# Matrix products of two feature blocks taken by turns, so that the PSUM bank changes

## The chip, the cores and the metric

The kernel runs on one core of a Trainium2 chip. The metric is the time of one execution on the device in microseconds (us), as the median of the runs shown. The engines of a core work side by side, each through its own queue in order: TensorE (PE in the profile; its weight loads are PEld), VectorE (DVE), ScalarE (ACT), GpSimd (POOL) and SyncE (SP), which issues the DMA transfers here. TensorE writes its products to PSUM, a memory of 8 banks in each partition, where they are summed.

## The reference

The reference is a decoder trunk of two layers on 256 positions of 1024 features, in float32. Cut to what matters:

```python
def swiglu(h, w_gate_up, w_down):
    a, b = jnp.split(h @ w_gate_up, 2, axis=-1)
    return (jax.nn.silu(a) * b) @ w_down

def hybrid_layer(x, ...):
    x = x + 0.5 * swiglu(rms_norm(x, ffn1_norm), ffn1_w_gate_up, ffn1_w_down)   # D_FF = 2816
    h = rms_norm(x, mix_norm)
    z = h @ w_in                                     # u, q, k, v and the logits gl of two gates
    u, q, k, v, gl = ...
    y_pool = multiscale_pool(u, pool_w, pool_scale)
    y_attn = moba_attention(rope(rms_norm(q)), rope(rms_norm(k)), v)            # 8 heads of 64
    gates = jax.nn.sigmoid(gl + b_gate).reshape(B, S, 2, D)
    merged = gates[:, :, 0] * (y_pool @ w_branch_pool) + gates[:, :, 1] * (y_attn @ w_branch_attn)
    x = x + merged @ w_out
    return x + 0.5 * swiglu(rms_norm(x, ffn2_norm), ffn2_w_gate_up, ffn2_w_down)
```

Nearly all of the work is in products of activations with weights that are read once.

## The kernel before

**Split operands.** Each float32 operand is split into a high part (rounded to the type that TensorE multiplies, float32r) and a low part (the rest, also float32r). A product of weights w and activations x is then hi(w)·hi(x) + hi(w)·lo(x) + lo(w)·hi(x). The activations' two parts lie side by side: `hx[:, k]` (also `hk[k]`) holds, for the feature block k of 128 features, 256 positions of the high part and then 256 positions of the low part. So one product with hi(w) and 512 moving columns gives two of the three terms, and one with lo(w) and 256 columns the third. In what follows they are the **high** and the **low** product. `chain` (L130) issues both, the high one into the whole of a PSUM bank (512 float32 in each partition), the low one into its first half, on top. At the end of a sum the two halves of the bank are added by `drain` (L157): ACT copies the second half (L158), and DVE adds the first (L159).

**Units.** The weights come in units of 128 x 2048, 16 blocks of 128 x 128. `unit()` (L91) starts the DMA of a unit into `raw` (4 buffers) and splits it in two halves of 8 blocks: for each half ACT writes hi (L112) and DVE writes lo (L113). There are six buffers for hi and six for lo, so three units fit, and a half's buffer is filled again once TensorE has read it for the last time. `blk(z, b)` picks the block b, in half 0 for b below 8 and in half 1 otherwise.

**Stages.** A layer is: a feed-forward stage (22 up units, then 11 down units), the mixing stage (tokens q, k, v, the projection u, 8 gate units with the attention between them, the branches, the output projection) and a second feed-forward stage. In an up unit the 16 blocks are two output blocks (j = 0 for the gate, j = 1 for the up part) times eight feature blocks k; the block is 2k + j. A gate unit has the same form, with the two gates as j. `pair` (L148) runs such a unit: it takes a PSUM tile `ps` of two banks, `ps[:, 0]` and `ps[:, 1]`, one for each j (there are two such tiles), goes over k and, within it, over j with `columns` (L142), and then drains. With `other` given, some other work is put between the first `at` feature blocks and the rest; that is so once in the first feed-forward stage and in the first gate of each layer. The first three up units of the kernel run together in `pairs` (L161), and in the other three feed-forward stages the first two up units are interleaved by hand; these do not go through `pair` without `other`.

In the down projection (L327 to L339) all 22 pairs of products of one output block go into one bank. The branches and the output projection use `chain3` (L135), three products of 256 columns for each block.

TensorE's instructions keep the order in which they are written (`mm`, L79, line 80 of the profile). The profile's line for all of them is L80, so the tiles tell them apart: `ps<-hx,hi` is a high product of an up, gate or u unit, `ps<-hx,lo` a low one, `ps<-ga,hi` and `ps<-gb,hi` belong to the down projection.

**Around it in the up projection.** For each unit DVE has two lo splits (L113), the drain's sum (L159), the scaling by the row factor (L322), the gate product (L325) and the low part of the result (L176); ACT has two hi splits (L112), the drain's copy (L158), the Silu (L324) and the high part of the result (L175).

Of the kernel before, what the change touches and what calls it, by code (L numbers as in the profile page):

```python
# [29 lines left out]
NK = D // P  # L30
# [19 lines left out]
def trunk_kernel(ctx: ExitStack, tc: tile.TileContext, x_in, w_in, pw_in, qkn_in, rope_in, mask_in, band_in, out):  # L50
# [28 lines left out]
    def mm(*args, **kw):  # L79
        return keep(nc.tensor.matmul(*args, **kw))  # L80

    def banks(pool, name):

        return pool.tile([P, 2, 2, S], F32, name=name, tag="mm" if pool is pmm else "at2")
# [30 lines left out]
    def blk(z, b, n=1):  # L115

        c = b * P % HALF
        return z[b * P // HALF][:, c:c + n * P]

    def steps(z):  # L120

        if len(z.shape) == 3:
            z = z.rearrange("p a s -> p (a s)")
        return z.rearrange("p (s a c) -> p a s c", a=4, c=4)

    def prod(ps, w, xk, first, last):

        return mm(steps(ps), lhsT=w, rhs=steps(xk), start=first, stop=last)

    def chain(ps, hi, lo, b, xk, first, last):  # L130

        prod(ps, blk(hi, b), xk, first, False)
        return prod(ps[:, 0, :], blk(lo, b), xk[:, 0, :], False, last)
# [8 lines left out]
    def columns(w, ps, ks):  # L142

        for k in ks:
            for j in range(2):
                chain(ps[j] if isinstance(ps, list) else ps[:, j], *w, 2 * k + j, hk[k], k == 0, k == NK - 1)

    def pair(w, t, other=None, at=0):  # L148

        ps = banks(pmm, "ps")  # L150
        columns(w, ps, range(at))
        if other:
            other()
        columns(w, ps, range(at, NK))
        drain(t, ps)

    def drain(t, ps):  # L157
        act(t, ps[:, :, 1, :], AF.Copy)  # L158
        tt(t, ps[:, :, 0, :], t, op=OP.add)  # L159
# [47 lines left out]
    hk = [hx[:, k] for k in range(NK)]  # L207
# [76 lines left out]
    def ffn(after, n0=0, end=False):  # L284
# [15 lines left out]
        if n0:  # L300
            pairs([unit() for _ in range(n0)], [wide() for _ in range(n0)])
            pair(unit(), wide(), sums, NK // 2)
        else:
            ws = [unit() for _ in range(2)]
            ts = [wide() for _ in range(2)]
            pss = [banks(pmm, "ps") for _ in range(2)]
            for u, k0, k1 in ((0, 0, NK - 1), (1, 0, 2), (0, NK - 1, NK), (1, 2, 4)):
                columns(ws[u], pss[u], range(k0, k1))
            drain(ts[0], pss[0])
            sums()  # L310
            columns(ws[1], pss[1], range(4, NK))
            drain(ts[1], pss[1])
        done = 0
        for i in range(n0 + 1 if n0 else 2, NF + 1):
            if i < NF:
                pair(unit(), wide())

            todo = range(done, min(done + 2, i) if i < NF else NF)
            done = todo.stop
            for j in todo:  # L320
                ab = abs_[j][1]
                tt(ab, ab, bc2(r[0]), op=OP.mult)  # L322
                sg = small.tile([P, S], F32, name="sg", tag="sg", bufs=2)
                act(sg, ab[:, 0, :], AF.Silu)  # L324
                tt(sg, sg, ab[:, 1, :], op=OP.mult)  # L325
                halves(gs[j], sg)
# [131 lines left out]
    def mix(l, after):  # L458
# [20 lines left out]
        def gate(f, *other):  # L479
            pair(unit(), gates[:, f], *other)  # L480
# [272 lines left out]
```

## Time and profile before

| | |
|---|---|
| median of 3 runs | 1010.97 us |
| lowest and highest run | 1008.93 and 1013.57 us |
| span of the profiled execution, first to last instruction | 1008.4 us |
| time of the profiled execution outside its span | not listed; the median of the runs lies 2.6 us above the span |
| TensorE, busy | 1001.3 us (99%), 6348 products |
| weight loads, busy | 905.9 us (90%) |
| DVE, busy | 795.9 us (79%) |
| ACT, busy | 626.1 us (62%) |
| HBM | 190 GB/s over the span |

A group's row reads: line, engine, operation, tile written and tiles read, shape, count, then busy us and the mean ns of one instruction, then the idle time of the engine just before them and what ended it. Products overlap in the array: one lasts 383 ns while the next starts 220 ns after it, so a count of starts per time says more than busy time. A row of the timeline has the start in us, the duration in us, engine, line, operation and tiles; in brackets the idle time before it and what ended that. A row of windows has the stretch, its length, and the busy time with the count of instructions for PE, PEld, DVE, ACT and POOL, then the granted clock of TensorE, the share of the DMA engines, and GB/s.

### The profile page before, as it was taken

How to read it: one execution, taken by the hardware profiler on the slowest of the kernel's cores; microseconds unless marked ns; L12 is line 12 of the kernel's file. 1: busy time of each engine (PE TensorE's matmuls, PEld its weight loads, DVE VectorE, ACT ScalarE, POOL GpSimd, SP SyncE). 2: the span in 40 equal slices, each digit the busy share in tenths (PEclk: the TensorE clock that was granted, in tenths of full speed). 3: DMA queues.
4: the chain of work that ended last, by engine and by line, in shares of the span. 5: the costliest groups of instructions: out<-in, count | busy, mean ns of one | idle time of the engine just before them, and what ended most of it. 6: DMA issues, size and time to landing. Idle time of an engine off the chain costs nothing.

```text
span 1008.4 us, 16031 instructions
## 1 busy us (share of the span) xinstructions
PE 1001.3 (99%) x6348; PEld 905.9 (90%) x6348; DVE 795.9 (79%) x1195; ACT 626.1 (62%) x985; POOL 1.4 (0%) x26
## 2 busy tenths in 40 slices
PE   8999999999999999999999999999999999999998
PEld 7889889898899998898898898898988998989987
DVE  7898866699769788886678888666998798888752
ACT  7966655567766766665576666556676567665641
POOL 0000000000000000000000000000000000000000
PEclk9999999999999999999999999999999999999999
DMA  8766566545526566656646565655544375656640
GB/s 290 272 229 218 180 209 209 192 156 169 204 84 227 192 209 209 209 174 206 206 168 211 206 209 175 207 203 186 189 167 147 118 255 173 228 181 209 207 148 22
DMA packets 30459, 192.91 MB, mean 191 GB/s; under 512 B 3376, under 2 KB 5680, under 8 KB 7856
## 3 DMA queue, kind: packets, MB, share of 16 engines
q1 hardware_dynamic: 30240, 191.71, 55.8%
q8 instruction: 50, 0.82, 0.3%
q10 hardware_dynamic: 144, 0.18, 0.1%
q14 instruction: 25, 0.20, 0.1%
HBM read 190.82 MB, written 1.05 MB: 190 GB/s over the span
## 4 chain that ended last, share of the span: by engine, by line
PE 84%; DVE 9%; ACT 3%; issue 2%; DMA 1%; SPq 0%; ACTq 0%; DVEq 0%
PE ps L80 73%; PE pt L80 6%; PE two L80 4%; DVE lo L113 3%; ACT hi L112 1%; DMA raw<-w 1%; DVE gates L159 1%; ACT pr L427 1%; DVE gates L483 1%; DVE nb L422 1%; DVE pr L432 1%; DVE sc L417 0%; ACT gates L486 0%; DVE gates L514 0%; DVE ab L322 0%
## 5 line engine op out<-in xcount | busy, mean ns | idle before, releaser
L80 PE MATMUL ps<-hx,hi 128*128 128x512 f32 x1712 | 574.8, 383 | 2.1 <-ACT hi L112 1.1
L113 DVE TENSOR_TENSOR lo<-raw,hi 128x1024 fp32r<-128x1024 f32 (+2 forms) x369 | 440.2, 1196 | 128.5 <-ACT hi L112 123.2
L112 ACT ACTIVATE hi<-raw 128x1024 fp32r<-128x1024 f32 (+2 forms) x369 | 379.3, 1035 | 219.0 <-PE ps L80 172.2
L80 PE MATMUL ps<-hx,lo 128*128 128x256 f32 x1712 | 467.8, 273 | 0.2 <-DVE lo L113 0.2
L80 PEld LDWEIGHTS ps<-hx,hi 128*128 128x128 f32 x1712 | 321.4, 188 | 60.9 <-DVE ab L159 1.7
L80 PEld LDWEIGHTS ps<-hx,lo 128*128 128x128 f32 x1712 | 321.7, 188 | 0.7 <-DVE lo L113 0.5
L80 PE MATMUL ps<-ga,hi 128*128 128x512 f32 (+1 forms) x528 | 172.4, 376 | 0.0
L80 PE MATMUL ps<-ga,lo 128*128 128x256 f32 x512 | 139.8, 273 | 0.0
L80 PEld LDWEIGHTS ps<-ga,hi 128*128 128x128 f32 x528 | 97.9, 188 | 16.6
L80 PEld LDWEIGHTS ps<-ga,lo 128*128 128x128 f32 x512 | 96.2, 188 | 0.0
L80 PE MATMUL ps<-gb,hi 128*128 128x512 f32 (+1 forms) x198 | 65.6, 376 | 0.0
L80 PE MATMUL pt<-hi,hx 128*128 128x512 f32 x192 | 65.1, 385 | 0.0
L322 DVE TENSOR_TENSOR ab<-ab,r 128x512 f32<-128x512 f32 x88 | 60.5, 691 | 2.4
L159 DVE TENSOR_TENSOR ab<-ps,ab 128x512 f32<-128x512 f32 x87 | 59.8, 687 | 2.2
L324 ACT ACTIVATE sg<-ab 128x256 f32<-128x256 f32 x88 | 36.6, 418 | 30.6 <-DVE ab L322 29.8
L80 PE MATMUL pt<-lo,hx 128*128 128x256 f32 x192 | 52.6, 274 | 0.0
L80 PE MATMUL ps<-gb,lo 128*128 128x256 f32 x192 | 52.4, 273 | 0.0
L158 ACT ACTIVATE ab<-ps 128x512 f32<-128x512 f32 x87 | 50.5, 580 | 0.3 <-PE ps L80 0.3
L175 ACT ACTIVATE ga<-sg 128x256 fp32r<-128x256 f32 x64 | 26.3, 418 | 36.4 <-DVE sg L325 35.2
L80 PE MATMUL two<-ax,hi 128*128 128x256 f32 x256 | 44.9, 278 | 0.1
L80 PE MATMUL ps<-ax,hi 128*128 128x256 f32 x256 | 44.1, 275 | 0.0
L80 PEld LDWEIGHTS ps<-gb,hi 128*128 128x128 f32 x198 | 36.7, 188 | 6.2
(148 smaller groups left out, 856.3 us busy)
## 6 DMA issues: line engine op xcount, KB each, us to landing
raw<-w SPq DMA_DIRECT2D x176, 1024.0 KB, 5.0
raw<-w SPq DMA_DIRECT2D x9, 256.0 KB, 6.2
raw<-w SPq DMA_DIRECT2D x2, 512.0 KB, 6.3
out_dram<-gx SPq DMA_DIRECT2D x8, 128.0 KB, 2.0
raw<-w SPq DMA_DIRECT2D x6, 128.0 KB, 3.7
gx<-x SPq DMA_DIRECT2D x3, 256.0 KB, 6.0
qk<-pw SPq DMA_DIRECT2D x2, 256.0 KB, 2.7
qkn<-qkn SPq DMA_DIRECT2D x1, 256.0 KB, 5.4
```

The costliest lines, as they stand in the source:

```text
L80: return keep(nc.tensor.matmul(*args, **kw))
L112: act(hi, w, AF.Copy)
L113: tt(lo, w, hi.bitcast(F32), op=OP.subtract)
L158: act(t, ps[:, :, 1, :], AF.Copy)
L159: tt(t, ps[:, :, 0, :], t, op=OP.add)
L175: act(d[:, 0, :], v, AF.Copy)
L322: tt(ab, ab, bc2(r[0]), op=OP.mult)
L324: act(sg, ab[:, 0, :], AF.Silu)
L422: nc.vector.tensor_reduce(nb[:, j, :], sc[:, :, c], axis=AX.X, op=OP.max)
L427: act(pr[:, h, c], sc[:, h, c], AF.Exp, scale=DH ** -0.5, bias=nb[:, j, h:h + 1], accum_out=su[:, j, h:h + 1])
L432: tt(pr[:, :, c], pr[:, :, c], su[:, j, :].unsqueeze(2).to_broadcast([P, 2, n]), op=OP.mult)
L483: tt(gates[:, f], gates[:, f], bc2(r), op=OP.mult)
```

## The change

Where `pair` has no `other`, the 32 products of a unit are issued in a new order by `turns`. The operands, the banks and the sums are the same. After the first high product of each bank, a high product of one block j is followed by a low product of the other block, one feature block behind: high(0,1), low(1,0), high(0,2), low(1,1), ... for three feature blocks, then the same with the blocks changed over, then both again for the second half of the unit's weights (four feature blocks each). The last two products are low. Within such a run each product goes to the other bank than the one before; where one run follows another, the last low product and the first high product share a bank.

```diff
     def pair(w, t, other=None, at=0):
 
         ps = banks(pmm, "ps")
-        columns(w, ps, range(at))
         if other:
+            columns(w, ps, range(at))
             other()
-        columns(w, ps, range(at, NK))
+            columns(w, ps, range(at, NK))
+        else:
+            turns(w, ps)
         drain(t, ps)
+
+    def turns(w, ps):
+
+        hi, lo = w
+
+        def high(j, k):
+            prod(ps[:, j], blk(hi, 2 * k + j), hk[k], k == 0, False)
+
+        def low(j, k):
+            prod(ps[:, j, 0, :], blk(lo, 2 * k + j), hk[k][:, 0, :], False, k == NK - 1)
+
+        h = NK // 2
+        high(0, 0)
+        high(1, 0)
+        for ks in (range(1, h), range(h, NK)):
+            for j in range(2):
+                for k in ks:
+                    high(j, k)
+                    low(1 - j, k - 1)
+        low(0, NK - 1)
+        low(1, NK - 1)
```

Written as high or low with (j, k), a unit was high(0,0), low(0,0), high(1,0), low(1,0), high(0,1), low(0,1), ...; it is now high(0,0), high(1,0), high(0,1), low(1,0), high(0,2), low(1,1), high(0,3), low(1,2), high(1,1), low(0,0), high(1,2), low(0,1), high(1,3), low(0,2), high(0,4), low(1,3), ..., high(0,7), low(1,6), high(1,4), low(0,3), ..., high(1,7), low(0,6), low(0,7), low(1,7).

## The prediction

> **What bounds the kernel now.** First the page: its busy shares, the clock line, the chain that ended last, and the two largest groups on TensorE.
>
> ```profile
> PE 1001.3 (99%) x6348; PEld 905.9 (90%) x6348; DVE 795.9 (79%) x1195; ACT 626.1 (62%) x985; POOL 1.4 (0%) x26
> PEclk9999999999999999999999999999999999999999
> PE 84%; DVE 9%; ACT 3%; issue 2%; DMA 1%; SPq 0%; ACTq 0%; DVEq 0%
> L80 PE MATMUL ps<-hx,hi 128*128 128x512 f32 x1712 | 574.8, 383 | 2.1 <-ACT hi L112 1.1
> L80 PE MATMUL ps<-hx,lo 128*128 128x256 f32 x1712 | 467.8, 273 | 0.2 <-DVE lo L113 0.2
> ```
>
> TensorE (PE) is busy 99% of the span at full granted clock, the chain that ended last is 84% PE, and the products that read hx waited 2.3 us in all. So a pair() unit can only become shorter if the pace of its products changes, and longer if that pace falls or if a new wait appears. The busy durations (383 and 273 ns) overlap, so the pace has to be read from starts, in the timeline of PE (start, duration, what):
>
> ```profile
> 94.63 0.38 PE L80 MATMUL ps<-hx,hi 128*128 128x512 f32 x1
> 94.85 0.27 PE L80 MATMUL ps<-hx,lo 128*128 128x256 f32 x1
> 94.96 0.38 PE L80 MATMUL ps<-hx,hi 128*128 128x512 f32 x1
> 95.18 0.28 PE L80 MATMUL ps<-hx,lo 128*128 128x256 f32 x1
> 95.29 0.38 PE L80 MATMUL ps<-hx,hi 128*128 128x512 f32 x1
> ...
> 149.96 0.38 PE L80 MATMUL ps<-ga,hi 128*128 128x512 f32 x1
> 150.18 0.27 PE L80 MATMUL ps<-ga,lo 128*128 128x256 f32 x1
> 150.29 0.38 PE L80 MATMUL ps<-ga,hi 128*128 128x512 f32 x1
> ```
>
> From a high product to the low one behind it 0.22 us, from a low one to the next high one 0.11: a pair takes 0.33 us. The upper rows (hx) are a pair() unit, in which the bank turns at each step from low to high. The lower rows (ga) are the down projection, in which 44 products in a row go to one bank. The steps look alike. Longer stretches make this sharp: pieces of the chain of waits cut out inside an up projection, inside a down projection, and the busy times by window (us, PE, PEld, DVE, ACT with counts, clock).
>
> ```profile
> 350.00 96.11 PE ps L80 x577
> ...
> 450.00 54.11 PE ps L80 x325
> ...
> core 0: us, PE busy (x) PEld busy (x) DVE busy (x) ACT busy (x) POOL busy (x), PEclk, DMA share, GB/s
> 295.00:320.00 25.00, 25.00 (x221) 25.00 (x220) 23.61 (x40) 15.39 (x24) 0.00 (x0) 1.00 0.49 168
> ...
> 346.00:448.00 102.00, 102.00 (x614) 91.78 (x614) 87.68 (x121) 65.28 (x99) 0.00 (x0) 1.00 0.60 201
> 448.00:506.00 58.00, 58.00 (x350) 52.21 (x350) 39.27 (x56) 32.15 (x47) 0.00 (x0) 1.00 0.58 195
> ```
>
> Between the first two rows the difference is 42.00 us for 252 products: 166.7 ns each, 333.3 a pair. Window by window, with the two products in flight at the edges taken off, the up projection has 102.00 / 612 = 166.7 ns and the down projection 58.00 / 348 = 166.7 ns. **So a bank turn at every second product gives the same pace as no turn at all.** This is the row on which the forecast rests. The window 295 to 320 holds only products of 256 columns, 25.00 / (221 - 2.5) = 114.4 ns each; the 512-column product then has 333.3 - 114.4 = 218.9.
>
> **The change part by part.** *Where it acts.* It acts in pair() without other(): units 4 to 21 of the first feed-forward stage (18), 20 units in each of the other three, and gates 1 to 7 of both layers (14). That is 92 units, 1472 pairs, 2944 of the 6348 products. Nothing is added or dropped: the same 32 products with the same operands, tiles, drains and loads in another order. No DMA is issued differently.
>
> *Turns.* Before, a unit has 15 turns among its 31 steps, all from low to high. Now it is 27: the two high ones at the start, 14 from high to low, 10 of 13 from low to high (at the ends of the three inner runs, low(1,2) to high(1,1) for instance, the bank stays), and low(0,7) to low(1,7). That is 12 more a unit, 1104 in all. The trace has no step from high to low with a turn, so its price is bounded. Nearest row, up against down: 0, known to about one product in 348 (0.5 ns a product, so about 1 ns a turn, 1.1 us in all). Far end: 2 x 114.4 - 218.9 = 9.9 ns of each product do not scale with its columns. If a turn hid all of this, 1104 x 9.9 = 10.9 us would go, and if it cost as much again, 10.9 us would come. I take 0, since the row of the same products with turns is the nearest.
>
> The Trainium skill, TensorE: Matmul & The Clock Gate, "Back-to-back issue gap", gives N / 2.4 + 2.5 ns for a product of N columns, 215.8 + 109.2 = 325.0 ns a pair. The 333.3 of the trace is 8.3 above it. If turns brought the page's figure, 1472 x 8.3 = 12.2 us would be gained, an estimate from that page. The same page says that a stream of weight loads and matmuls is set by both, and the trace agrees as far as it goes, with PEld busy all 25.00 us where the products have 256 columns.
>
> *The order of the halves.* With 218.9 and 114.4 ns a step, the first use of hi[1], high(0,4), comes 8 high and 6 low products into the unit, at 2.44 us instead of 2.67. First uses of lo[0] and lo[1] move from 0.22 to 0.66 and from 2.89 to 2.99. The refills run far ahead, so the 0.23 us costs nothing. By the rows below, the hi split at 103.18 refills what the unit begun at 100.29 releases, three units ahead of its use at 116.3. In the ramp after the start (40 to 58 us) PE waits for drains, whose place at the end of a unit is the same.
>
> *The release that moves.* The last read of lo[0] was the eighth pair's, from 2.55 us of the unit on. Now it is low(0,3), product 24, which starts behind 13 high and 10 low ones: 13 x 0.2189 + 10 x 0.1144 = 3.99 us. With its 0.27 us, lo[0] is free at 4.26 us, 1.4 later. The buffer's next writer is DVE's split (L113), in order with everything else on DVE.
>
> ```profile
> 97.71 1.06 ACT L112 ACTIVATE hi<-raw 128x1024 fp32r<-128x1024 f32 x1 [1.12 <-PE ps L80]
> 98.81 1.23 DVE L113 TENSOR_TENSOR lo<-raw,hi 128x1024 fp32r<-128x1024 f32 x1
> ...
> 100.29 0.38 PE L80 MATMUL ps<-hx,hi 128*128 128x512 f32 x1
> 101.34 0.69 DVE L159 TENSOR_TENSOR ab<-ps,ab 128x512 f32<-128x512 f32 x1
> 103.18 1.04 ACT L112 ACTIVATE hi<-raw 128x1024 fp32r<-128x1024 f32 x1
> 104.26 1.23 DVE L113 TENSOR_TENSOR lo<-raw,hi 128x1024 fp32r<-128x1024 f32 x1
> 107.95 0.68 DVE L159 TENSOR_TENSOR ab<-ps,ab 128x512 f32<-128x512 f32 x1
> ...
> 94.96:100.29 5.33, 5.33 (x34) 4.79 (x33) 4.19 (x6) 3.02 (x4) 0.00 (x0) 1.00 0.73 271
> 100.29:105.62 5.33, 5.33 (x34) 4.79 (x33) 4.72 (x8) 3.64 (x6) 0.00 (x0) 1.00 0.41 125
> ```
>
> Units start at 94.96 and 100.29. Today the two splits of lo[0] start at 98.81 and 104.26, as soon as hi is there. With the release at 94.96 + 4.26 = 99.22 and 100.29 + 4.26 = 104.55 they start 0.41 and 0.29 us later. Queued behind them on DVE are the gate product (L325), its halves (L176), the next drain (L159) and L322. DVE's idle time in two units is 10.66 - 4.19 - 4.72 = 1.75 us, more than the 0.70 added. The drain at 101.34, or 101.75 when late, ends by 102.5, and its PSUM banks are wanted at 105.63; the one at 107.95 would end by 109.1 and is wanted at 110.96. So PE does not see it: 0 us.
>
> The gates are where DVE has least room. There the chain runs over DVE, and the window 230 to 286 has PE full. Here is a gate unit's start and the split that refills its lo[0]:
>
> ```profile
> 230.00:286.00 56.00, 55.95 (x383) 49.32 (x383) 48.56 (x80) 40.83 (x85) 0.00 (x0) 1.00 0.50 170
> ...
> 250.15 0.38 PE L80 MATMUL ps<-hx,hi 128*128 128x512 f32 x1
> ...
> 255.59 1.22 DVE L113 TENSOR_TENSOR lo<-raw,hi 128x1024 fp32r<-128x1024 f32 x1
> ```
>
> The new release, 250.15 + 4.26 = 254.41, is still 1.2 us before this split, and the other gates have at least as much. Nothing moves there.
>
> *Ends.* Both drains wait for the unit's last product, which is a low one at the same time as before; two high ones at the start and three low ones at the end change no sum of steps.
>
> **Sum**: 1104 turns x 0 + 0 for the first uses + 0 for the release = 0. The profiled span is 1008.4 us; the runs have 1008.93 to 1013.57 with a median of 1010.97, 2.6 us above that span. So 1008.4 for a profile of the changed kernel, and 1011.0 for its median. About 0.5% (5 us) is what a measurement of this kernel can tell from no change.
>
> **The rivals.**
>
> 1. *A turn from high to low hides part of the fixed time* (chance 0.17). For it: 9.9 ns a product that columns do not explain, and that no row shows this step with a turn. The equality of up and down could also come from a weight load that fills the low product's 114 ns whether the bank turns or not (PEld is full where all products are low-sized), and then only the high product has room. Against it: the equality itself. At half the bound, 5.5 us go and the time is 1005.5; at all of it, 1000.1. Faster by over 0.5% needs 4.6 ns or more a turn.
>
> 2. *The late release of lo[0] makes DVE the bound* (chance 0.08, slower). The mechanism is L113 in DVE's queue, in the up projections. It decides once the time that it waits is no longer absorbed by the 1.75 us of idle in two units, because the idle itself is waiting for ACT (0.5 and 1.0 us pieces) that shifts along. Then each unit lasts 0.35 us longer (half of 0.70), once the drains have used their room of 110.96 - 108.63 = 2.3 us, after 7 units. With some 13 units left in each of four stages, 52 x 0.35 = 18 us: 1029. Against it: hi[1] is free 0.23 us earlier, so ACT's part shrinks too.
>
> 3. *A turn costs* (chance 0.04, slower). At the far bound 10.9 us: 1022. Up against down speaks against it.
>
> 4. *PE drops to half pace* (chance 0.01). The warm-up products show what half pace is beside later ones of the same shape:
>
> ```profile
> 1.05 2.29 PE L80 MATMUL busy<-ones 128*128 128x128 f32 x9 [1.05 <-DVE eps L191]
> ...
> 218.73 1.03 PE L399 MATMUL tp<-ident,q 128*128 128x128 f32 x8
> ```
>
> (2.29 - 0.43) / 8 = 0.23 us a step against (1.03 - 0.27) / 7 = 0.11. The 1472 pairs at twice 0.333 us would add 490 us: 1500. A PE that is full has nothing to bring this on; all windows above have clock 1.00. The Trainium skill, TensorE: Matmul & The Clock Gate, "A second HAM failure mode: psum-queue depth-cycling", tells of a kernel whose cycling through PSUM banks left small idle pieces and made the clock go back and forth. By that rule more turns would be a loss; the trace, at clock 1.00 with 15 turns a unit, does not agree so far.
>
> 5. *The change does less than it says*: 4 of 31 steps keep their bank, and 53% of the products are outside. That only scales rival 1 and is in its numbers.
>
> **How the numbers follow.** No change 0.70, rival 1 0.17, rival 2 0.08, rival 3 0.04, rival 4 0.01. Predicted 1011.0. The forecast's own range is 1008 to 1014, the runs' spread and the 1.1 us of the nearest row. For 8 in 10 it is widened to 1003 on the side of rival 1 (some two thirds of its chance), and to 1016 on the slow side, for a small drain wait. Faster by over 0.5%: most of rival 1 and a little spread, 0.16. Slower: rivals 2, 3 and 4 and a little spread, 0.13, less what of rival 3 stays under 5 us: 0.12. Within: 0.72.
>
> **What would show it.** In the changed profile's up projections, 32 products should take 5.33 us, as now, with high to low 0.22 us and low to high 0.11. Rival 1 would show 0.21 or so for the step from high to low in another bank, and a unit of about 5.27. L113 should have a new wait for PE of 0.3 to 0.4 us at every lo[0] split in the steady part of the up projections, some 60 times, and the wait for ACT ahead of the following L113 (0.99 us) should be shorter. PE should have no wait longer than before. Should PE wait for DVE (L159) inside an up projection, rival 2 is right; should the clock be under 1.00, rival 4; should the step from high to low be over 0.23, rival 3. The forecast is wrong if the unit's length differs from 5.33 us by more than 0.05.

## The result, and the profile after

The changed kernel takes 1018.78 us (median of 7 runs, 1016.36 to 1019.84) against 1010.97 us before (7 runs, 1008.59 to 1015.11). The ratio is 1.0072, with a 95% interval of 1.0053 to 1.0091: **slower by 0.7%**, some 8 us, outside the forecast range of 1003 to 1016.

The page of the changed kernel, the lines that answer to those of before:

```profile
PE 1011.2 (99%) x6348; PEld 910.6 (89%) x6348; DVE 794.6 (78%) x1195; ACT 630.1 (62%) x985; POOL 1.4 (0%) x26
PEclk9999999999999999999999999999999999999999
PE 98%; DMA 1%; SPq 0%; DVE 0%; ACT 0%; issue 0%
L80 PE MATMUL ps<-hx,hi 128*128 128x512 f32 x1712 | 568.8, 387 | 1.6 <-ACT hi L112 1.6
L80 PE MATMUL ps<-hx,lo 128*128 128x256 f32 x1712 | 441.7, 275 | 0.2 <-DVE lo L113 0.2
```

PE is as full as before, has no new wait inside the stages, and is busy 9.9 us longer with the same 6348 products. A high product lasts 387 ns on average instead of 383, a low one 275 instead of 273. So nothing is late: the products themselves come more slowly. Where, is seen in the windows of the changed kernel that the prediction read in the kernel before (stretch, length, PE with count, PEld, DVE, ACT, POOL, clock, DMA share, GB/s):

```profile
346.00:448.00 102.00, 102.00 (x600) 90.31 (x599) 85.56 (x119) 66.30 (x100) 0.00 (x0) 1.00 0.58 195
448.00:506.00 58.00, 58.00 (x350) 52.12 (x349) 39.68 (x55) 32.24 (x47) 0.00 (x0) 1.00 0.56 193
```

In the up projection 102.00 / (600 - 2) = 170.6 ns a product instead of 166.7; in the down projection, which the change does not touch, 58.00 / 348 = 166.7 as before. The clock is 1.00 in both.

The starts of the products in the trace give the length of each unit (32 products, us):

| 20 units of pair() in a row | before | changed |
|---|---|---|
| layer 0, second feed-forward | all 5.333 | all 5.460 |
| layer 1, first feed-forward | all 5.333 | 5.461, 5.354, 5.466, 5.354, ... |
| layer 1, second feed-forward | all 5.333 | all 5.460 |

In the first feed-forward stage, which has 18 such units, all last 5.460 in the changed kernel. Before, they last 5.333 from the sixth on, and some of the first five more, up to 5.953.

Stage by stage, against a second profile of the kernel before (the run "before again" below, span 1009.3 us, where the first unit of pair() also starts 31.5 us into the span, against 29.3 in the first profile), the sum is: the four up projections +1.69, +2.53, +1.53 and +2.53 us, the gates +0.47 and +0.46, the stretches around them -0.96, together +8.25 us. The down projections have the same length to 0.01 us.

Within a slow unit the steps no longer repeat every two pairs. From the trace's starts, in ns (H is a high product and the time to the next start, L a low one):

```
before:  H221 L111 H222 L113 H221 L111 H222 L113 ...              333.3 a pair
changed: H225 L113 H232 L117 H224 L115 H225 L113 H232 L117 ...    342.0 a pair
```

The same slow sequence stands in the trace of the kernel **before**, in the old order, at the head of the second feed-forward stage, where the first two units are interleaved by hand. Its timeline of PE (start, duration, what):

```profile
331.87 0.39 PE L80 MATMUL ps<-hx,hi 128*128 128x512 f32 x1
332.10 0.27 PE L80 MATMUL ps<-hx,lo 128*128 128x256 f32 x1
332.21 0.39 PE L80 MATMUL ps<-hx,hi 128*128 128x512 f32 x1
...
333.93 0.39 PE L80 MATMUL ps<-hx,hi 128*128 128x512 f32 x1
334.15 0.27 PE L80 MATMUL ps<-hx,lo 128*128 128x256 f32 x1
```

From 331.87 to 333.93 lie six pairs: 343 ns each (342 over the last twelve pairs of the stretch, by the exact starts), with no wait and no turn from high to low. The second feed-forward stage of layer 1 begins in the same way. This stretch ends with the two products of the row sums. It led to theory B of the experiments: a regular alternation of 512- and 256-column products runs at one of two paces, 333.3 or 342 ns a pair, and keeps the one it is in; products of one size in a row can move it from one to the other. In the changed kernel each unit's border has them. Three low and three high products in a row, from its timeline:

```profile
528.02 0.38 PE L80 MATMUL ps<-hx,hi 128*128 128x512 f32 x1
528.24 0.50 PE L80 MATMUL ps<-hx,lo 128*128 128x256 f32 x3
528.58 0.84 PE L80 MATMUL ps<-hx,hi 128*128 128x512 f32 x3
```

Theory A is that of rival 3: a turn from high to low costs about 9 ns. Both fit the time, since a unit has 14 such turns and 14 x 9 = 126 ns.

### The profile page after: what moved, and what is told of

Its sections match the earlier page's. It is cut to its first block, busy times and chain, and to the rows that moved or that the text cites. A ratio compares the mean times of both kernels' runs of the same rounds, so it can differ in the third digit from the quotient of the medians.

```text
span 1017.5 us, 16066 instructions
## 1 busy us (share of the span) xinstructions
PE 1011.2 (99%) x6348; PEld 910.6 (89%) x6348; DVE 794.6 (78%) x1195; ACT 630.1 (62%) x985; POOL 1.4 (0%) x26
## 4 chain that ended last, share of the span: by engine, by line
PE 98%; DMA 1%; SPq 0%; DVE 0%; ACT 0%; issue 0%
PE ps L80 84%; PE pt L80 7%; PE two L80 4%; PE sc L80 1%; PE pt L462 1%; DMA raw<-w 1%; PE pe L80 0%; PE tp L422 0%; SPq L667 0%; PE yp L80 0%; PE y L80 0%; PE st L80 0%; PE ss L80 0%; SPq L664 0%; DVE lo L113 0%; ACT hi L112 0%
## 5 line engine op out<-in xcount | busy, mean ns | idle before, releaser
L80 PE MATMUL ps<-hx,hi 128*128 128x512 f32 x1712 | 568.8, 387 | 1.6 <-ACT hi L112 1.6
L113 DVE TENSOR_TENSOR lo<-raw,hi 128x1024 fp32r<-128x1024 f32 (+2 forms) x369 | 440.5, 1196 | 120.2 <-ACT hi L112 118.8
L112 ACT ACTIVATE hi<-raw 128x1024 fp32r<-128x1024 f32 (+2 forms) x369 | 380.2, 1037 | 248.1 <-PE ps L80 201.9
L80 PE MATMUL ps<-hx,lo 128*128 128x256 f32 x1712 | 441.7, 275 | 0.2 <-DVE lo L113 0.2
L80 PEld LDWEIGHTS ps<-hx,hi 128*128 128x128 f32 x1712 | 315.2, 188 | 60.2 <-ACT hi L112 1.9
L80 PEld LDWEIGHTS ps<-hx,lo 128*128 128x128 f32 x1712 | 315.4, 188 | 7.6 <-DVE lo L113 0.5
L348 DVE TENSOR_TENSOR sg<-sg,ab 128x256 f32<-128x256 f32 x88 | 36.9, 424 | 36.4 <-ACT sg L347 36.4
```

Source lines behind the costliest of these rows:

```text
L112: act(hi, w, AF.Copy)
L113: tt(lo, w, hi.bitcast(F32), op=OP.subtract)
```

## The experiments

Each kernel replaces the body of `turns` in the changed kernel, unless something else is said. The lengths of units are from the starts of products in the profiled run.

### Turns without the rhythm: alternate

```diff
-        (the list of the change)
+        columns(w, ps, range(1))
+        for ks in (range(1, NK // 2), range(NK // 2, NK)):
+            for j in range(2):
+                for k in ks:
+                    high(j, k)
+                    low(1 - j, k)
```

(The flag that ends a bank's sum is moved to its new last product.)

> High and low products strictly by turns, as before the change, but from the second feature block on each low product goes to the other bank than the high product ahead of it: 14 turns from high to low in a unit, as in the changed kernel. Theory A (a turn from high to low costs about 9 ns): a unit lasts 5.46 us, the time is about 1019. Theory B (PE has two paces for high and low by turns, 333.3 and 342 ns a pair; it keeps the one it is in, and two high or two low products in a row can move it from one to the other; banks do not matter): nothing moves it inside the stages, a unit lasts 5.33 us, the time is about 1011.

Measured: 1011.42 us against 1010.94, ratio 1.0005 (0.9988 to 1.0021). All 60 units in the three later up projections last 5.333 us. The window of layer 0's second feed-forward stage, in this run and in the kernel before:

```profile
350.00:430.00 80.00, 80.00 (x481) 72.00 (x480) 68.60 (x96) 51.22 (x78) 0.00 (x0) 1.00 0.60 206
```

```profile
350.00:430.00 80.00, 80.00 (x482) 71.98 (x482) 68.59 (x95) 50.98 (x78) 0.00 (x0) 1.00 0.60 201
```

80.00 / 479 = 167.0 ns against 80.00 / 480 = 166.7, the pace of before to one product in 480. Fourteen turns from high to low in each unit cost nothing. Theory A falls here.

### The rhythm without turns: rhythm

```diff
                     high(j, k)
-                    low(1 - j, k - 1)
+                    low(j, k - 1)
```

> The changed kernel's rhythm of high and low products (three high ones at the start of a unit, three low ones at its end, one feature block between a high product and the low one behind it), but each low product goes to the bank of the high one ahead of it: no turn from high to low. Theory A: 5.33 us a unit, about 1011. Theory B: as the changed kernel, 5.46 us a unit in most stages, 1017 to 1019.

Measured: 1017.27 us, ratio 1.0063 (1.0037 to 1.0088), nearly that of the change. The same window:

```profile
350.00:430.00 80.00, 80.00 (x471) 70.88 (x470) 66.84 (x92) 51.18 (x77) 0.00 (x0) 1.00 0.59 201
```

80.00 / 469 = 170.6 ns. The units are 5.460 in the second feed-forward stages and 5.461, 5.354, 5.466, 5.354 ... in layer 1's first, as in the changed kernel to a nanosecond or two. The loss comes whichever banks the products go to. These two runs settle the question of the banks, on which the prediction turned.

They do not quite single out the order of sizes: alternate also puts each low product back on the feature block of the high one ahead of it, and rhythm leaves it one block behind, as the change does. That lag is not the cause either. The units of 5.354 us in the changed kernel have it and run nearly at the old pace, and two high, below, loses the time without it.

### Two in a row at the head of a unit: head

```diff
+        high(0, 0)
+        high(1, 0)
+        low(0, 0)
+        low(1, 0)
+        columns(w, ps, range(1, NK))
```

> The order of before, except that the first four products of a unit are high, high, low, low. Theory A: one turn from high to low in a unit, 9 ns, so 92 x 0.009 = 0.8 us more, about 1012. Theory B: the two products in a row can move PE to the other pace for the whole rest of the unit; which way is not known, so whole units last either 5.33 us or about 5.33 + 14 x 0.009 = 5.46, and the time lies between 1011 and 1023, with units of both lengths or of the long one alone as its sign.

Measured: 1011.18 us, ratio 0.9998 (0.9985 to 1.0011). Theory B gave a range here and its low end came out. In the second feed-forward stages all units last 5.333. In layer 1's first stage they are 5.484, 5.365, 5.333, 5.333, ..., and the first feed-forward stage begins alike (5.483, 5.365). The steps around the first head of a stage, in ns, with the head between bars:

```
layer 0, second: ... H221 L111 H222 L113 | H221 H220 L113 L110 | H223 L111 H222 L113 ...                     stays fast
layer 1, first:  ... L114 H221 L110 | H222 H219 L119 L117 | H227 L113 H237 L116 H228 L118 H225 L114 H232 ... becomes slow
```

In layer 1's first stage PE comes to the first head in the fast pace and leaves it in the slow one, and the second head brings it back. So the same head, high, high, low, low, can leave the fast pace alone, end it, or end the slow one. The range of theory B left room for this, units of both lengths among them. Not every repetition does harm.

### Two and two throughout: twos

```diff
+        for k in range(NK):
+            high(0, k)
+            high(1, k)
+            low(0, k)
+            low(1, k)
```

> Two high products and then two low ones for every feature block, without a long run by turns. Theory A: 8 turns from high to low in a unit, 72 ns, 92 x 0.072 = 6.6 us more, 1017.6. Theory B: neither of the two paces is kept; by the steps of the changed kernel (high to high 220 ns, high to low 222 to 234, low to low 109, low to high 116) four products take 667 to 679 ns, a unit 5.34 to 5.43 us, the time 1011 to 1020, and every unit has the same length.

Measured: 1022.02 us, ratio 1.0095 (1.0071 to 1.0119), but not for the reason of either theory. In the middle of the three later up projections the units last 5.333 us again (H223 H220 L113 L110, some 667 ns for four products). The time goes in the down projections, 1.7 to 3.0 us each, and at the ends of the up projections. The down projections of layer 0's second stage and layer 1's first run at the slow pace (7.53 us for 44 products instead of 7.33), which is some 1.4 us of their 3.0. The rest is waiting. From the waits of PE and the timeline of DVE:

```profile
PE ps L80 <- DVE gb L194: 5.5, 4, 1.4
...
66.24 0.43 DVE L194 TENSOR_TENSOR ga<-sg,ga 128x256 fp32r<-128x256 f32 x1 [0.48 <-ACT ga L193]
...
71.69 0.42 DVE L194 TENSOR_TENSOR ga<-sg,ga 128x256 fp32r<-128x256 f32 x1 [0.48 <-ACT ga L193]
...
77.15 0.42 DVE L194 TENSOR_TENSOR ga<-sg,ga 128x256 fp32r<-128x256 f32 x1 [0.48 <-ACT ga L193]
```

The instructions of DVE and ACT stand in another order in their queues here, though nobody asked for it: only PE's order is written by hand, and the others are put between. DVE now waits for ACT twice a unit and needs 5.45 us for it (66.24, 71.69, 77.15), more than PE's 5.33. It falls behind by 0.12 us a unit until PE waits for the last results (gb) of the stage. This is the mechanism of rival 2, by another cause. Together with the slow down projections it keeps this run from saying more than that PE's own units were 5.333.

### Slow pace in the old kernel, on purpose: two high

In the kernel of before, once at the head of each of the three later feed-forward stages:

```diff
             sums()
+            dm = quarter("dm")
+            prod(dm, one_r, hk[0], True, True)
+            prod(dm, one_r, hk[0], True, True)
             columns(ws[1], pss[1], range(4, NK))
```

> The kernel of before, banks and order unchanged, with two more 512-column products into a bank that nobody reads, once at the head of each of the three later feed-forward stages, behind the two products of the row sums (so low, low, low, high, high, high, as at the border of two units in the changed kernel). Six more products in 6348. Theory A (turns from high to low cost): 6 x 0.22 = 1.3 us, 1012. Theory B (two paces, kept by strict alternation): the group puts PE into the slow pace, and the alternation that follows keeps it there through 20 up units (5.48 us each instead of 5.33) and the down projection (342 ns a pair instead of 333.3): some 500 pairs x 9 ns = 4.5 us a stage, 13.6 + 1.3 in all, 1026. If the slow pace ends at the border to the down projection, 8.8 + 1.3, 1021.

Measured: 1021.56 us against 1011.52, ratio 1.0099 (1.0067 to 1.0131): 10 us for six products that take 1.3 us. Windows of its profile, in the first feed-forward stage, the second one's up and down projections, and layer 1's first:

```profile
70.00:120.00 50.00, 50.00 (x294) 44.20 (x293) 41.79 (x57) 30.53 (x47) 0.00 (x0) 1.00 0.57 191
350.00:430.00 80.00, 80.00 (x469) 70.72 (x468) 67.99 (x94) 50.59 (x78) 0.00 (x0) 1.00 0.56 187
460.00:500.00 40.00, 40.00 (x236) 35.34 (x235) 26.41 (x37) 21.60 (x32) 0.00 (x0) 1.00 0.56 189
530.00:610.00 80.00, 80.00 (x482) 71.97 (x481) 68.68 (x96) 52.79 (x81) 0.00 (x0) 1.00 0.58 195
```

The second feed-forward stage runs at 80.00 / 467 = 171.3 ns through all 20 units (5.472 to 5.483 us) and through its down projection (40.00 / 234 = 170.9). Its order and banks are those of before. Against the second profile of the old kernel this stage is 2.84 + 1.57 us longer. The pace, once there, stays for over 160 us until something breaks the alternation. Here PE comes to the group in the slow pace, as in the kernel before, where the two products of the row sums alone turn it fast; with the two high ones behind them it stays slow. Two things came out otherwise than expected. The group did this in one stage of three: layer 1's first stage runs at 80.00 / 480 = 166.7 behind it and its second at the same pace (5.333 us a unit). By the trace, PE came to the group slow and left it fast in the one, and came fast and left fast in the other. So the 1021 of the expectation was met by other terms than it names. And the *first* stage, which is not edited, is slow in this execution too (50.00 / 292 = 171.2; it adds 1.96 + 1.57 us, so some of the 10 us are not the group's).

### The control: high low

The same with a 512- and a 256-column product:

```diff
+            prod(dm, one_r, hk[0], True, True)
+            prod(dm[:, 0, :], one_r, hk[0][:, 0, :], True, True)
```

> The same with a 512-column and a 256-column product in place of the two 512-column ones, so that high and low stay in turn: low, low, low, high, low, high. Both theories: 3 x 0.33 = 1.0 us more than before, 1012, up units of 5.33 us. It shows that the added products themselves, their bank and their place cost no more than their own time.

Measured: 1012.59 us, ratio 1.0013 (0.9996 to 1.0030). All units of the three stages last 5.333, so added products of both sizes in turn cost their own time. This is the closest comparison of the case: in layer 0's second stage PE comes to the group in the slow pace, at the same point of its repetition, in the kernel before, in two high and here, and only with two high ones in a row is it slow behind it. The unedited first stage of high low is slow, as in two high:

```profile
70.00:120.00 50.00, 50.00 (x294) 44.19 (x293) 40.61 (x56) 31.25 (x48) 0.00 (x0) 1.00 0.56 192
350.00:430.00 80.00, 80.00 (x482) 71.98 (x481) 68.93 (x97) 51.72 (x79) 0.00 (x0) 1.00 0.59 199
```

### A lag of one product: lag one

```diff
+        high(0, 0)
+        for k in range(NK):
+            high(1, k)
+            low(0, k)
+            if k + 1 < NK:
+                high(0, k + 1)
+            low(1, k)
```

> The low products lag by one step in the list, so that a unit is high(0,0), high(1,0), low(0,0), high(0,1), low(1,0), ... high(1,7), low(0,7), low(1,7): 15 turns from high to low in a unit, but only two high products at the start and two low ones at the end. Theory A: 15 x 9 ns x 92 = 12.4 us more, 1023. Theory B: the pace depends on the border low, low, high, high alone; whole units last 5.33 us if it leaves PE in the fast pace (1011), or 5.46 if not (1018). A result of 1011 rules out theory A a second time.

Measured: 1020.98 us, ratio 1.0086 (1.0054 to 1.0118). By its time alone it would sit between both theories. Its units in the three later up projections are 5.471 and 5.349 by turns, not 5.46 throughout: each border low, low, high, high moves PE to the other pace. Every unit has the same 15 turns from high to low, and half of the units have the loss and half have next to none, which theory A cannot give. A part of the time is again DVE's queue, for which PE waits 2.3 us (gb), and the first and last down projections, 3.1 and 1.7 us longer, run at the slow pace too (7.53 us for 44 products).

### The head in the first stage alone, and the kernel of before again

In the kernel of before, units 10 to 21 of the first stage take the head high, high, low, low:

```diff
-                pair(unit(), wide())
+                pair(unit(), wide(), head=n0 and i > 9)
```

> The order of before, but in the first feed-forward stage alone units 10 to 21 begin high, high, low, low. In the runs of two other kernels the first stage, which is not edited there, lay in the slow pace (5.47 us a unit) and kept it to the end of its down projection; in the run with this head in every unit a slow stage came back to 5.33 us within two heads. Theory B (two paces): where an execution of the kernel of before comes into the slow pace in its first stage it loses up to 12 x 0.14 + 1.6 = 3.3 us behind unit 10, and this kernel gets that back; in the other executions nothing changes. So the profile shows 5.33 us a unit from unit 12 on, the median is 0 to 3 us below that of before, and a verdict clear of noise is not sure. Theory A: 12 x 9 ns = 0.1 us more, no difference.

Measured: 1010.96 us against 1011.33, ratio 0.9995 (0.9983 to 1.0008): no difference that can be measured. Its profile caught what it was made for: units 8 and 9 last 5.578 and 5.483 us, unit 10, the first with the head, 5.365, and all later ones 5.333. One head was enough to end the slow pace. The highest of its 12 runs is 1012.00; the highest of the 17 of before beside it is 1014.91. That fits a first stage that is slow in some executions only, but with one profile each it is not shown.

> The kernel of before once more, for a second profile of the same instructions. Theory B: all stages behind the first as in the first profile; the first stage in one of the two paces, 5.33 or 5.47 us a unit in its later units, by chance of the waits ahead of it. Theory A: 5.33 us in all units.

> A third profile of the kernel of before, with the same expectations: the first stage in one pace or the other, the later stages as in the first profile.

Measured: 1011.33 and 1011.39 us, one run each. The later up projections are those of the first profile to the nanosecond, and the first stage came to 5.333 in both. So none of three profiles of the old kernel is slow in its first stage. The profiles that are belong to two high, high low and, up to unit 9, this one, whose products there are the same.

## Why the prediction was wrong

**The step that failed** is the sentence under *Ends*: "two high ones at the start and three low ones at the end change no sum of steps". Their own steps hardly change, but they choose the pace of the products between them. The prediction took 333.3 ns a pair as fixed by the products, and it is one of two paces. This term was put at 0. It measured 127 ns a unit in three of the four up projections, 77 on average in layer 1's first, and some 67 in a gate. Less the 0.59 us by which three units of the first stage were longer in that profile of the old kernel, and the 0.96 around the stages, that is the 8.25 us above.

**Turns** were put at 0, from up against down, and that is what they cost: alternate has 14 of them from high to low in a unit and the time of before. The rhythm without them has the time of the change. Rival 3 gave 1022 and its time was nearly right for a wrong reason; a forecast that had taken it would have been no better founded. Its bound was too wide as well. The prediction took the low product's 114.4 ns from another stage, which left 9.9 ns of each product that do not scale with its columns; by the steps of the up projection itself, 221.2 and 112.1 ns on average, it is 2 x 112.1 - 221.2 = 3.0. Rival 1 falls by alternate too: no turn hides any of the time that does not scale with columns.

**What was to be seen beforehand.** The profile of before held the slow pace, from 330.5 us, for 24 pairs. The prediction read long windows and the one number for the waits (2.3 us) and took the rest to be uniform. The windows that it read begin at 346 and 350, behind that stretch. Two short windows at the stage's head, or the mean duration of a high product there (387 ns against 382), would have shown that the same products have two paces.

**First uses and drains**: right. PE has no wait for a weight's half or a drain inside the changed units, and the gates hold the window 230 to 286 without a gap.

**The late release of lo[0]**: no PE time, as forecast, but its sign did not come. L113 waits for PE once in the whole trace (0.8 us, in the attention) and never in an up projection. The waits of the changed kernel, with the one of before to compare:

```profile
ACT hi L112 <- PE ps L80: 201.9, 212, 3.7
DVE lo L113 <- ACT hi L112: 118.8, 166, 2.8
...
PE ps L80 <- ACT hi L112: 1.6, 1, 1.6
```

```profile
ACT hi L112 <- PE ps L80: 172.2, 151, 3.7
```

ACT's waits for PE went from 172.2 to 201.9 us. The queues of ACT and DVE also stand in another order in the changed kernel, arranged around PE's; how much of the difference is due to that was not measured. The prediction had kept their order fixed, which was a second error; it cost nothing here. In twos and lag one it did.

**Rival 4**, half pace by a gated clock, has no row for it: 1.00 in the windows of the slow stages. The Trainium skill, TensorE: Matmul & The Clock Gate, "A second HAM failure mode: psum-queue depth-cycling", tells of a loss from cycling through PSUM banks, by way of short idle pieces of TensorE and a clock that goes back and forth. Here PE has no idle pieces in these stages, and in alternate more turns come without a loss and at a clock of 1.00, so the trace shows nothing of it. Its "Back-to-back issue gap" gives figures that, at full clock, go by the number of columns alone; here the same 512 columns take 220 to 222 ns in one pace and 224 to 233 in the other, so the trace does not agree with that.

**What stays open** is why there are two paces. In the traces a weight load begins 2 to 3 ns behind the start of the product ahead of it, in the slow pace as in the fast, and no wait is listed, so the order of issue shows no difference.

Which way a border moves PE was only observed, but in the traces it goes by the point of the repetition at which the border comes. Told by the last step from a low to a high product ahead of the border, in the traces of the changed kernel, rhythm, two high, head and the run with the head in the first stage:

| border | pace before, last such step | pace behind | borders |
|---|---|---|---|
| three low, three high | slow, 113 ns | slow | 94 of 94 |
| three low, three high | slow, 117 ns | fast | 35 of 35 |
| three low, three high | fast, 113 ns | slow | 32 of 32 |
| three low, three high | fast, 111 ns | fast | 1 of 1 |
| high, high, low, low | fast, 113 ns | fast | 91 of 91 |
| high, high, low, low | fast, 111 ns | slow | 2 of 2 |
| high, high, low, low | slow, 117 ns | fast | 3 of 3 |

(Steps to a nanosecond or so.) This orders what looked like chance: two high, whose group is such a border of three and three, stayed slow behind 113, turned fast behind 117, and stayed fast behind 111. It is a count after the fact that no run was made to test, and it gives the pace only where the steps ahead of a border are known.

## What to carry to other kernels

Where TensorE is the bound and its products are of two sizes, the order of sizes can be worth more than banks: count starts per microsecond stage by stage, in short windows, and treat a stage at another pace as a finding, not as waits. A border between groups should keep the alternation that is known to run fast, or be tried with the profile beside it. And an order written by hand for one engine can reorder the queues of the others; compare those too before putting a time on them.

## What was not expected of the hardware

A stream of 512- and 256-column products by turns, each with its own weights, has two stable paces on the same core at a granted clock of 1.00: 333.3 ns a pair, repeating every two pairs, and 342, repeating every three. It stays in either for as long as the alternation lasts, 160 us in one run, over the changes of tiles, banks and operands between an up and a down projection. Two added products of 0.22 us each were enough to keep a stage slow that is fast without them, and the later units of the first stage were found in either pace with the same products (5.333 us in the kernel of before, 5.47 with two high and with high low). The turns between PSUM banks cost less than can be seen: 14 from high to low in each of 92 units left the ratio at 1.0005 (0.9988 to 1.0021).
